# A hybrid decoder layer: score matmuls of differential attention on half-height stacks

## The chip, the cores and the metric

The kernel runs on one core of a Trainium2 chip. The metric is the device time of one execution in microseconds (us), given as the median of the runs.

## What is computed

One decoder layer over 1024 tokens of width 1024, all in float32. The rows are normalised, projected by one matrix `w_in`, and split among two groups of four heads. Group A is causal differential attention: each head has two components `c` with queries and keys of 64 features, two softmaxes, and the difference of the two weighs the values. Group B is retention in chunks of 128 tokens. The heads' outputs are normalised, gated, projected by `w_out`, normalised again and added to the input. The part that the change touches:

```python
s = jnp.einsum('bhcqd,bhckd->bhcqk', qb, kf)      # d = 64, c = 2 components
s = jnp.where(causal, s, jnp.float32(-1e30))
p = jax.nn.softmax(s, axis=-1)
a = p[:, :, 0] - lam * p[:, :, 1]
return jnp.einsum('bhqk,bhkv->bhqv', a, vf)
```

## The kernel before, in words

To keep float32 accuracy, most operands are split into a high part (rounded to the matmul's operand type) and a low part (the rest). The projections multiply high by high, high by low and low by high: three matmuls in `proj_rows` (L296 to L298, 256 columns each) and in `proj_cols` (L308 to L310, 512 columns each).

The projections run block by block: 16 blocks of 256 columns of `w_in`, each in four groups (`main_group`). After each group the program emits other work of the heads ("side" functions): `attend(i)` of a differential head, which is `diff_scores` of query tile i and `diff_values` of tile i - 1, over the eight groups of two blocks; and `ret_chunks` of a retention head. A planner then orders the instructions of every engine by when it expects their operands and buffers to be ready, so the score matmuls stand between projection matmuls of later blocks. The order on an engine is fixed after that.

`diff_qk` makes the rotated queries and keys of one head, transposed: features in rows, tokens in columns. The tiles `hi` and `lo` (L373, L374) hold the parts, the queries' two components in rows 0-31 and 32-63, the keys' in 64-95 and 96-127, for the two rotary halves `r`. Sixteen transfers from SP (`mv`, L384 and L385) for each half of the tokens copy them into the stacks `st["q"]` and `st["k"]`. A stack has four row blocks of 32 for each component `u` and rotary half `r`: the queries as high, high, low, low, the keys as high, low, high, low. One matmul over the 128 rows thus adds all four products for one `r`, and two matmuls (L399, r = 0 and 1) make the scores of one component.

`diff_scores` for tile i has n = (i + 1) * 128 keys: one piece up to 512 keys, two equal pieces above. Each piece of each component takes one bank of the pool `ps_s` (3 banks). DVE finds the largest score (L403 with the mask, L408 without), ACT takes the exponential (L413) and so frees the bank, and DVE subtracts the two components (L426). `diff_values` transposes the difference (L444) into banks of the pool `ps_m` (`pm`, 3 banks), ACT copies them out (L447), and the matmuls L449 apply them to the values, in a `pm` bank that is held until the output is gated (`emit_y`, L343). `ret_chunks` uses three `pm` tiles in turn, and so do the transposes at the start (`norm_tile`, L278) and before the output projection (`prep_tile`, L566). The output projection (`out_tile`, L585 to L587) writes to banks of `ps_s` and of `ps_j` in turn.

Of the kernel before, what the change touches and what calls it, by code (L numbers as in the profile page):

```python
# [10 lines left out]
F32 = mybir.dt.float32  # L11
F32R = mybir.dt.float32r
# [5 lines left out]
PSUM = bass.MemoryType.PSUM  # L18
# [12 lines left out]

# Column layout of the constants that depend on shapes alone.
C_FREQ = 0
# [6 lines left out]

# Heads (differential 0-3, retention 4-7) and the order of their blocks of w_in:
# part 0 holds the values and gates, part 1 the queries and keys.
HEADS = [0, 4, 1, 5, 2, 6, 3, 7]
# [4 lines left out]
def shape_constants():  # L48
    c = np.zeros((P, NCST), np.float64)
    c[:, C_FREQ:C_FREQ + 64] = THETA ** (-np.arange(64) / 64.0)  # L50
    t = np.arange(S).reshape(NT, P).T
    for h in range(H):
        # Retention by g^(i-j) is g^(i+1) times a sum over values scaled by g^-(j+1).
        g = 1.0 - 2.0 ** (-5.0 - h)
        c[:, C_VSC + h * NT:C_VSC + (h + 1) * NT] = g ** (-(t + 1.0)) * 128.0 ** -0.5
        c[:, C_OSC + h * NT:C_OSC + (h + 1) * NT] = g ** (t + 1.0)
        c[:, C_RSC + h * NT:C_RSC + (h + 1) * NT] = g ** (t + 1.0) * 128.0 ** -0.5
    c[:64, C_QSC] = 64.0 ** -0.5
    c[64:, C_QSC] = 1.0
    return c.astype(np.float32)  # L60


def two_pi_parts():
    """1/(2 pi) times powers of two, modulo 1, in parts that multiply whole numbers exactly."""
    from fractions import Fraction

    inv = Fraction(1) / Fraction(
        "6.28318530717958647692528676655900576839433879875021164194988918461563281257")

    def turn(power):  # L70
        t = inv * power
        t -= round(t)
        return t

    def part(t, bits):
        q = Fraction(round(t * 2 ** bits), 2 ** bits)
        return float(q), t - q

    a = turn(2 ** 16)
    a1, r = part(a, 8)  # L80
    a2, r = part(r, 16)
    a3 = float(r)
    b = turn(2 ** 4)
    b1, r = part(b, 12)
    b2 = float(r)
    return a1, a2, a3, b1, b2, float(inv)


def body(ctx, tc, x, pos, wpk, wout, vecs, npre, npost, subln, cst, out):
# [18 lines left out]
    ps_j = pool("ps_j", 2, space=PSUM)  # L108
    ps_s = pool("ps_s", 3, space=PSUM)
    ps_m = pool("ps_m", 3, space=PSUM)  # L110

# [8 lines left out]

# [1 line left out]
    cs = const.tile([P, NCST], F32, name="cs")  # L122
# [9 lines left out]
    def rsqrt(dst, src, more):  # L132
        """(src + more) ** -0.5"""
        nc.vector.tensor_scalar(dst, src, more, None, op0=ALU.add)  # L134
        nc.gpsimd.tensor_tensor(dst, dst, halves[:, 0:dst.shape[-1]], op=ALU.pow)  # L135

# [1 line left out]
    NB = 16  # L138
    lo_turn = [0]

    def split_lo(dst, full, hi):
        """dst = full - hi, rounded to the tensor engine's operand (exact)."""
        lo_turn[0] += 1
        eng = nc.vector if lo_turn[0] % 4 in (2, 3) else nc.gpsimd
        eng.tensor_tensor(dst, full, hi.bitcast(F32), op=ALU.subtract)  # L145

    def load_chunk(b, c, staging=None):
        """A quarter of a block."""
        raw = (staging or wraw).tile([P, 2, 256], F32, tag="raw", name="raw")
        nc.sync.dma_start(raw, wpk[b, :, 2 * c:2 * c + 2, :])  # L150
        hi = whi.tile([P, 2, 256], F32R, tag="whi", name="whi")
        nc.scalar.copy(hi, raw)  # L152
        lo = wlo.tile([P, 2, 256], F32R, tag="wlo", name="wlo")
        split_lo(lo, raw, hi)
        return hi, lo
# [6 lines left out]

# [1 line left out]
    HT = S // 2  # L164
# [9 lines left out]
    def angles(tp, posi):  # L174
        """cos and sin of position * frequency, with an exact reduction to one turn."""
        a1, a2, a3, b1, b2, inv = two_pi_parts()
# [27 lines left out]
        nc.vector.tensor_tensor(C, C, B, op=ALU.subtract)  # L204
        # small parts first
        nc.vector.tensor_scalar(acc, A, a3 * 2.0 ** -16, None, op0=ALU.mult)
# [6 lines left out]
        frac(acc, acc, t2)  # L213
        # cos x = sin(x + a quarter turn)
        nc.vector.tensor_scalar(t1, acc, 0.25, None, op0=ALU.add)
# [69 lines left out]
    def proj_rows(w, t2):  # L285
        """Two token tiles of u @ block: [tok, 2, 256]."""
        ps = pj()
        for j in range(2):
            t = 2 * t2 + j
            dst = ps[:, j * 256:(j + 1) * 256]  # L290
            cols = slice(t % 4 * P, (t % 4 + 1) * P)
            for kt in range(KT):
                wh, wl = weight(w, kt)
                a = uh[t // 4][:, kt, cols]
                b = ul[t // 4][:, kt, cols]
                nc.tensor.matmul(dst, lhsT=a, rhs=wh, start=(kt == 0 and j == 0), stop=False)  # L296
                nc.tensor.matmul(dst, lhsT=a, rhs=wl, start=False, stop=False)  # L297
                nc.tensor.matmul(dst, lhsT=b, rhs=wh, start=False, stop=(kt == KT - 1 and j == 1))  # L298
        return ps.rearrange("p (j f) -> p j f", j=2)

    def proj_cols(w, f, half):
        """128 features of the block over 512 tokens, transposed."""
        ps = pj()
# [30 lines left out]
    def emit_y(st, t, o_ps, tot):  # L334
        """The head's output, normalised and gated, to its columns of y."""
        hh, gt = st["h"], st["g"]
# [10 lines left out]

# [1 line left out]
    dp = {}  # L349
# [4 lines left out]
    def diff_qk(st, w, g):  # L354
        """Step g of 4: features (first, second rotary halves) of each half of the tokens."""
        half, f = g // 2, g % 2
        if g == 0:
            st["q"] = dp["stk"].tile([P, 2, 2, S], F32R, tag="qs", name="qs")
            st["k"] = dp["stk"].tile([P, 2, 2, S], F32R, tag="ks", name="ks")
        sl = slice(half * HT, (half + 1) * HT)  # L360
# [14 lines left out]
        for r, o in enumerate((o1, o2)):  # L375
            nc.scalar.copy(hi[:, r, :], o)
            split_lo(lo[:, r, :], o, hi[:, r, :])
        for u in range(2):
            for b in range(4):
                rows = slice(b * 32, (b + 1) * 32)  # L380
                q0, k0 = u * 32, 64 + u * 32
                sq = hi if b < 2 else lo
                sk = hi if b % 2 == 0 else lo
                mv(st["k"][rows, u, :, sl], sk[k0:k0 + 32, :, :])  # L384
                mv(st["q"][rows, u, :, sl], sq[q0:q0 + 32, :, :])  # L385

    def diff_scores(st, i):
        n = (i + 1) * P
        pieces = [(0, n)] if n <= 512 else [(0, n // 2), (n // 2, n // 2)]
        np_ = len(pieces)  # L390
        probs, sums = [], []
        for u in range(2):
            nm = sm_.tile([P, 2], F32, tag="nm", name="nm")
            banks = []
            for b, (k0, kn) in enumerate(pieces):
                last = b == np_ - 1
                sp = ps_s.tile([P, 512], F32, tag="sc", name="sc")
                for r in range(2):
                    nc.tensor.matmul(sp[:, 0:kn], lhsT=st["q"][:, u, r, i * P:(i + 1) * P],  # L399
                                     rhs=st["k"][:, u, r, k0:k0 + kn], start=(r == 0), stop=(r == 1))  # L400
                if last:
                    # -(scores with the mask), and the least of it
                    nc.vector.tensor_tensor_reduce(  # L403
# [3 lines left out]
                else:  # L407
                    nc.vector.tensor_reduce(nm[:, 0:1], sp[:, 0:kn], axis=AX.X, op=ALU.max, negate=True)  # L408
                banks.append(sp)
            p = dp["pp"].tile([P, S], F32, tag="p", name="p")  # L410
            ss = sm_.tile([P, 2], F32, tag=f"ss{u}", name="ss")
            for b, (k0, kn) in enumerate(pieces):
                nc.scalar.activation(p[:, k0:k0 + kn], banks[b][:, 0:kn], AF.Exp,  # L413
                                     scale=-1.0 if b == np_ - 1 else 1.0,
                                     bias=nm[:, np_ - 1:np_], accum_out=ss[:, b:b + 1])
# [40 lines left out]

# [1 line left out]
    def ret_qk(st, w, t2):  # L458
# [63 lines left out]

# [1 line left out]
    fp = {}  # L524
# [8 lines left out]
    def split_wout(nh, ms):  # L533
        """Rows of w_out for half nh of the columns, scaled by what y was not yet scaled by."""
        for m in ms:
# [63 lines left out]

# [1 line left out]
    heads = [{"h": hh} for hh in HEADS]  # L601
# [53 lines left out]

    # Blocks in the order of their weights, and what follows each group of four.
    def attend(i):
# [63 lines left out]
def pack(inputs):  # L721
    """The inputs, laid out for the program's loads."""
    w = np.asarray(inputs["w_in"])[0]
# [49 lines left out]
```

## Time and profile before

| what | value |
|---|---|
| median of 3 runs | 607.66 us (607.46 to 608.18) |
| span of the profiled execution, first to last instruction | 606.4 us |
| TensorE (PE) busy | 588.3 us, 97% |
| VectorE (DVE) busy | 324.4 us, 53% |
| ScalarE (ACT) busy | 236.1 us, 39% |
| GpSimd (POOL) busy | 140.7 us, 23% |
| mean granted clock of TensorE | 0.999 of full speed |

The profile gives the span of its execution; the execution's own time is not listed apart from those of the timed runs, whose median lies 1.3 us above the span. PE are the matmuls, PEld the loads of their stationary operand, which run beside them. Successive matmuls overlap in the profile, so their durations add up to more than the time that they take; the chain of work that ended last, which follows each step back to what released it, gives each matmul only the time that it added.

### The profile page before, as it was taken

What the parts mean: (1) busy time and instruction counts of PE and PEld (TensorE: products, weight loads), DVE (VectorE), ACT (ScalarE), POOL (GpSimd) and SP (SyncE); (2) the same over time, 40 slices, a digit from 0 to 9 for tenths busy, and PEclk for the clock granted to TensorE, in tenths of its full rate; (3) what the DMA queues carried; (4) which work ended last, traced back from release to release, by engine and by line L of the source; (5) the groups of instructions that cost most, each with busy time, mean ns of one, the idle gap of its engine ahead of it and who ended that gap; (6) DMA issues with size and microseconds to landing.
All of it is one profiled execution on the core that took longest, in us unless ns stands there. A gap on an engine that the chain in (4) does not pass through costs nothing.

```text
span 606.4 us, 10873 instructions
## 1 busy us (share of the span) xinstructions
PE 588.3 (97%) x4144; PEld 552.3 (91%) x4144; DVE 324.4 (53%) x820; ACT 236.1 (39%) x652; POOL 140.7 (23%) x171
## 2 busy tenths in 40 slices
PE   4999999999999999999999999999999999999995
PEld 3999989999989999999899998899999988888884
DVE  4888335755654357723444556456566673343232
ACT  5643522444433343534134445223546443212110
POOL 4303124411224032313241102343310230000000
PEclk9999999999999999999999999999999999999999
DMA  8602237510228420202185202482202372332221
GB/s 298 237 2 71 70 69 174 161 33 22 76 59 224 92 80 9 79 10 78 37 189 152 79 10 78 92 222 66 67 27 79 112 272 62 122 119 76 91 69 71
DMA packets 36196, 59.66 MB, mean 98 GB/s; under 512 B 4784, under 2 KB 12208, under 8 KB 36144
## 3 DMA queue, kind: packets, MB, share of 16 engines
q1 hardware_dynamic: 36000, 58.70, 33.0%
q8 instruction: 33, 0.54, 0.3%
q10 hardware_dynamic: 144, 0.26, 0.1%
q14 instruction: 19, 0.16, 0.1%
HBM read 34.30 MB, written 7.86 MB: 70 GB/s over the span
## 4 chain that ended last, share of the span: by engine, by line
PE 95%; DVE 1%; DMA 1%; issue 1%; ACT 0%; POOL 0%; SPq 0%; DVEq 0%; POOLq 0%; ACTq 0%
PE pj L296 15%; PE pj L298 15%; PE pj L297 15%; PE sc L399 6%; PE pm L449 5%; PE pj L308 5%; PE pj L310 5%; PE pj L309 5%; PE pm L444 3%; PE pj L585 2%; PE op L585 2%; PE pj L587 2%; PE pj L586 2%; PE op L587 2%; PE op L586 2%; PE pm L566 1%
## 5 line engine op out<-in xcount | busy, mean ns | idle before, releaser
L296 PE MATMUL pj<-whi,uh 128*128 128x256 f32 x768 | 221.6, 289 | 1.0 <-ACT uh L281 1.0
L298 PE MATMUL pj<-whi,ul 128*128 128x256 f32 x768 | 221.1, 288 | 0.5 <-DVE ul L282 0.5
L297 PE MATMUL pj<-wlo,uh 128*128 128x256 f32 x768 | 219.9, 286 | 0.0
L296 PEld LDWEIGHTS pj<-whi,uh 128*128 128x128 f32 x768 | 148.1, 193 | 2.1 <-ACT uh L281 1.6
L298 PEld LDWEIGHTS pj<-whi,ul 128*128 128x128 f32 x768 | 148.0, 193 | 1.0 <-DVE ul L282 0.8
L297 PEld LDWEIGHTS pj<-wlo,uh 128*128 128x128 f32 x768 | 148.1, 193 | 0.6
L135 POOL TENSOR_TENSOR tot<-tot,halves 128x1 f32<-128x1 f32 (+1 forms) x56 | 34.5, 616 | 275.3 <-DVE tot L134 273.2
L413 ACT ACTIVATE p<-sc,nm 128x384 f32<-128x384 f32 (+5 forms) x96 | 55.1, 580 | 53.8 <-DVE nm L403 52.5
L145 POOL TENSOR_TENSOR wlo<-raw,whi 128x512 fp32r<-128x512 f32 x32 | 46.4, 1453 | 78.5 <-ACT whi L152 68.8
L152 ACT CAST whi<-raw 128x512 fp32r<-128x512 f32 x64 | 39.4, 623 | 34.3 <-PE pj L309 17.5
L308 PE MATMUL pj<-uh,whi 128*128 128x512 f32 x128 | 50.5, 394 | 0.0
L309 PE MATMUL pj<-ul,whi 128*128 128x512 f32 x128 | 50.4, 394 | 0.0
L310 PE MATMUL pj<-uh,wlo 128*128 128x512 f32 x128 | 50.2, 392 | 0.0
L399 PE MATMUL sc<-ks,qs 128*128 128x384 f32 (+5 forms) x192 | 46.1, 346 | 0.0
L449 PE MATMUL pm<-v,at 128*128 128x128 f32 x288 | 39.7, 275 | 0.0
L447 ACT COPY at<-pm 128x512 f32<-128x512 f32 (+3 forms) x48 | 23.1, 481 | 42.4 <-PE pm L444 42.3
L449 PEld LDWEIGHTS pm<-v,at 128*128 128x128 f32 x288 | 36.8, 192 | 0.6
L145 DVE TENSOR_TENSOR wlo<-raw,whi 128x512 fp32r<-128x512 f32 x32 | 26.1, 827 | 19.9 <-ACT whi L152 19.0
L343 DVE SCALAR_TENSOR_TENSOR y<-pm,tot,gt 128x128 f32<-128x128 f32 x56 | 18.4, 348 | 24.9 <-POOL tot L135 16.6
L399 PEld LDWEIGHTS sc<-ks,qs 128*128 128x128 f32 x192 | 30.5, 191 | 1.0
L403 DVE CUSTOM_DVE_ANT_0 sc<-sc,mask,nm 128x320 f32<-128x320 f32 (+3 forms) x32 | 21.0, 655 | 18.8 <-PE sc L399 18.6
L434 ACT ACTIVATE sq<-pm,cs 128x128 f32<-128x128 f32 x32 | 11.4, 363 | 47.5 <-PE pm L511 47.4
(145 smaller groups left out, 971.5 us busy)
## 6 DMA issues: line engine op xcount, KB each, us to landing
raw<-in_wpk SPq DMA_DIRECT2D x64, 256.0 KB, 3.4
xt<-in_x SPq DMA_DIRECT2D x15, 512.0 KB, 3.8
ks<-rhi SPq DMA_DIRECT2D x32, 128.0 KB, 2.4
qs<-rhi SPq DMA_DIRECT2D x32, 128.0 KB, 2.4
ks<-rlo SPq DMA_DIRECT2D x32, 128.0 KB, 2.4
qs<-rlo SPq DMA_DIRECT2D x32, 128.0 KB, 2.4
raw<-in_wout SPq DMA_DIRECT2D x16, 256.0 KB, 3.0
out<-ob SPq DMA_DIRECT2D x16, 256.0 KB, 2.4
```

The source lines that it names most:

```text
L135: nc.gpsimd.tensor_tensor(dst, dst, halves[:, 0:dst.shape[-1]], op=ALU.pow)
L145: eng.tensor_tensor(dst, full, hi.bitcast(F32), op=ALU.subtract)
L152: nc.scalar.copy(hi, raw)
L296: nc.tensor.matmul(dst, lhsT=a, rhs=wh, start=(kt == 0 and j == 0), stop=False)
L297: nc.tensor.matmul(dst, lhsT=a, rhs=wl, start=False, stop=False)
L298: nc.tensor.matmul(dst, lhsT=b, rhs=wh, start=False, stop=(kt == KT - 1 and j == 1))
L308: nc.tensor.matmul(ps, lhsT=wh, rhs=uh[half][:, kt, :], start=(kt == 0), stop=False)
L309: nc.tensor.matmul(ps, lhsT=wh, rhs=ul[half][:, kt, :], start=False, stop=False)
L310: nc.tensor.matmul(ps, lhsT=wl, rhs=uh[half][:, kt, :], start=False, stop=(kt == KT - 1))
L399: nc.tensor.matmul(sp[:, 0:kn], lhsT=st["q"][:, u, r, i * P:(i + 1) * P], rhs=st["k"][:, u, r, k0:k0 + kn], start=(r == 0), stop=(r == 1))
L413: nc.scalar.activation(p[:, k0:k0 + kn], banks[b][:, 0:kn], AF.Exp, scale=-1.0 if b == np_ - 1 else 1.0, bias=nm[:, np_ - 1:np_], accum_ou ...
L449: nc.tensor.matmul(o_ps[:, 0:P], lhsT=at[:, j * P:(j + 1) * P], rhs=v[:, j0 + j, :], start=(j0 + j == 0), stop=(j0 + j == i))
```

## The change

The stacks hold each part once: four tiles of 128 rows by 1024 tokens (queries high, queries low, keys high, keys low), with component 0 in rows 0-63 and component 1 in rows 64-127, both rotary halves within these. There are still 16 transfers for each half of the tokens, of half the size. The scores of one component are now three matmuls over its 64 rows (high by high, low by high, high by low; the product of the low parts is left out), and the matmuls of the two components alternate, each component in a bank of its own. For each piece of the keys both components are now done before the next piece; the exponentials follow behind all of the maxima. The pool `ps_s` has 4 banks in place of 3, and `ps_m` 2 in place of 3. The rest of the diff is comments.

```diff
-    ps_s = pool("ps_s", 3, space=PSUM)
-    ps_m = pool("ps_m", 3, space=PSUM)
+    ps_s = pool("ps_s", 4, space=PSUM)
+    ps_m = pool("ps_m", 2, space=PSUM)
...
         if g == 0:
-            st["q"] = dp["stk"].tile([P, 2, 2, S], F32R, tag="qs", name="qs")
-            st["k"] = dp["stk"].tile([P, 2, 2, S], F32R, tag="ks", name="ks")
+
+            for n in ("qh", "ql", "kh", "kl"):
+                st[n] = dp["stk"].tile([P, S], F32R, tag=n, name=n)
...
-        for u in range(2):
-            for b in range(4):
-                rows = slice(b * 32, (b + 1) * 32)
-                q0, k0 = u * 32, 64 + u * 32
-                sq = hi if b < 2 else lo
-                sk = hi if b % 2 == 0 else lo
-                mv(st["k"][rows, u, :, sl], sk[k0:k0 + 32, :, :])
-                mv(st["q"][rows, u, :, sl], sq[q0:q0 + 32, :, :])
+        for n, src in (("h", hi), ("l", lo)):
+            for r in range(2):
+                for u in range(2):
+                    rows = slice(64 * u + 32 * r, 64 * u + 32 * r + 32)
+                    mv(st["q" + n][rows, sl], src[32 * u:32 * u + 32, r, :])
+                    mv(st["k" + n][rows, sl], src[64 + 32 * u:96 + 32 * u, r, :])
...
+        qs = slice(i * P, (i + 1) * P)
+        nms, banks = [], ([], [])
         for u in range(2):
-            nm = sm_.tile([P, 2], F32, tag="nm", name="nm")
-            banks = []
-            for b, (k0, kn) in enumerate(pieces):
-                last = b == np_ - 1
-                sp = ps_s.tile([P, 512], F32, tag="sc", name="sc")
-                for r in range(2):
-                    nc.tensor.matmul(sp[:, 0:kn], lhsT=st["q"][:, u, r, i * P:(i + 1) * P],
-                                     rhs=st["k"][:, u, r, k0:k0 + kn], start=(r == 0), stop=(r == 1))
+            nms.append(sm_.tile([P, 2], F32, tag="nm", name="nm"))
+        for b, (k0, kn) in enumerate(pieces):
+            last = b == np_ - 1
+            sps = [ps_s.tile([P, 512], F32, tag="sc", name="sc") for u in range(2)]
+            terms = (("qh", "kh"), ("ql", "kh"), ("qh", "kl"))
+            for m, (qn, kn_) in enumerate(terms):
+                for u in range(2):
+                    rows = slice(64 * u, 64 * u + 64)
+                    nc.tensor.matmul(sps[u][:, 0:kn], lhsT=st[qn][rows, qs], rhs=st[kn_][rows, k0:k0 + kn],
+                                     start=(m == 0), stop=(m == 2))
+            for u in range(2):
+                sp, nm = sps[u], nms[u]
...
-                banks.append(sp)
+                banks[u].append(sp)
+        for u in range(2):
+            nm = nms[u]
             p = dp["pp"].tile([P, S], F32, tag="p", name="p")
...
-                nc.scalar.activation(p[:, k0:k0 + kn], banks[b][:, 0:kn], AF.Exp,
+                nc.scalar.activation(p[:, k0:k0 + kn], banks[u][b][:, 0:kn], AF.Exp,
```

## Rows read from the trace of the kernel before

**Rows 1.** Page, busy time of each engine, share of the span, instructions.

```profile
PE 588.3 (97%) x4144; PEld 552.3 (91%) x4144; DVE 324.4 (53%) x820; ACT 236.1 (39%) x652; POOL 140.7 (23%) x171
```

**Rows 2.** Page, the chain that ended last, by engine and by line.

```profile
PE 95%; DVE 1%; DMA 1%; issue 1%; ACT 0%; POOL 0%; SPq 0%; DVEq 0%; POOLq 0%; ACTq 0%
PE pj L296 15%; PE pj L298 15%; PE pj L297 15%; PE sc L399 6%; PE pm L449 5%; PE pj L308 5%; PE pj L310 5%; PE pj L309 5%; PE pm L444 3%; PE pj L585 2%; PE op L585 2%; PE pj L587 2%; PE pj L586 2%; PE op L587 2%; PE op L586 2%; PE pm L566 1%
```

**Rows 3.** What PE waited for: us in total, times, longest.

```profile
PE pm L278 <- DVE xu L272: 8.0, 2, 7.1
...
PE pm L486 <- ACT qkT L483: 0.6, 1, 0.6
```

**Rows 4.** Score matmuls by shape, whole kernel: busy us, mean ns.

```profile
L399 PE MATMUL sc<-ks,qs 128*128 128x512 f32 x48 | 14.6, 403 | 0.0
...
L399 PE MATMUL sc<-ks,qs 128*128 128x128 f32 x16 | 2.5, 257 | 0.0
```

**Rows 5.** The chain in order of time: start us, us, what; steps of each width.

```profile
by line: PE pj L296 15.0%; PE pj L298 15.0%; PE pj L297 15.0%; PE sc L399 5.6%; PE pm L449 5.3%; PE pj L308 4.8%; PE pj L310 4.8%; PE pj L309 4.8%; PE pm L444 2.6%; PE pj L585 2.4%; PE op L585 2.4%; PE pj L587 2.4%; PE op L587 2.4%; PE pj L
...
103.50 0.48 PE sc L399 x4
110.07 0.70 PE sc L399 x4
...
126.19 0.88 PE sc L399 x6
...
135.77 1.04 PE sc L399 x6
...
194.20 0.40 PE sc L399 x4
194.59 0.17 PE pj L296
...
214.07 0.93 PE sc L399 x4
...
452.27 1.22 PE sc L399 x6
...
463.29 1.39 PE sc L399 x6
```

**Rows 6.** Weight loads and matmuls in time, 193.9 to 194.6 us, 128-column scores.

```profile
193.92 0.54 PEld L399 LDWEIGHTS sc<-ks,qs 128*128 128x128 f32 x4
194.37 0.19 PEld L296 LDWEIGHTS pj<-whi,uh 128*128 128x128 f32 x1
...
194.03 0.56 PE L399 MATMUL sc<-ks,qs 128*128 128x128 f32 x4
```

**Rows 7.** PE in time, 159.8 to 160.5 us, transposes then projection.

```profile
159.83 0.60 PE L444 MATMUL pm<-ident,p 128*128 128x128 f32 x4
160.18 0.48 PE L309 MATMUL pj<-ul,whi 128*128 128x512 f32 x1
160.50 0.40 PE L310 MATMUL pj<-uh,wlo 128*128 128x512 f32 x1
```

**Rows 8.** ACT copy by shape; engines from 480 us; the chain near 496 us.

```profile
L447 ACT COPY at<-pm 128x512 f32<-128x512 f32 x24 | 14.1, 587 | 17.5 <-PE pm L444 17.4
...
480.00:500.00 20.00, 18.57 (x158) 18.18 (x157) 15.62 (x35) 10.60 (x24) 6.72 (x10) 1.00 0.67 231
...
496.39 0.37 ACT sq L434
...
499.89 0.66 PE pm L566 x4
```

**Rows 9.** One stack's transfers (KB, us to landing); waits for the staging tiles.

```profile
ks<-rhi SPq DMA_DIRECT2D x32, 128.0 KB, 2.4
...
DVE rlo L145 <- DMA qs<-rlo: 7.6, 2, 4.3
...
ACT rhi L376 <- DMA ks<-rhi: 6.2, 2, 3.5
```

## The prediction

> **What bounds the kernel now.** I read the engine totals first [rows 1]: TensorE (PE) is busy 588.3 us of a span of 606.4, every other engine at most 53%. Busy is not bound by itself, so the chain of waits comes next [rows 2]: 95% of the chain that ended last is PE, and the score matmuls (L399) have 6% of it (the same chain in order of time says 5.6%, that is 34.0 us [rows 5]). The last view is what PE waited for [rows 3]: its largest entry is 8.0 us in two waits at the start, for a normalised tile; in the middle of the kernel it practically never waits, because projection matmuls of the next blocks fill every hole. So a microsecond of PE's own work, added or removed between 97 and 472 us, should show in the end nearly one for one. A faster transfer or a faster DVE there should show as nothing.
>
> All prices below come from the one profiled execution (span 606.4). The three timed runs have a median of 607.66, so 1.3 us lie around the span; I add differences to 607.66.
>
> **What a score matmul costs today.** The mean durations in the table by shape (403 ns at 512 columns) [rows 4] are not prices: successive matmuls overlap. The price is the share on the chain [rows 5]: four of 512 columns take 0.93 us, six take 1.39, so 0.232 each; 448: 1.22/6 = 0.203; 384: 1.04/6 = 0.173, or 0.70/4 = 0.175; 320: 0.88/6 = 0.147; 256: 0.48/4 = 0.12. For 128 columns the row says 0.40 for four, but the projection matmul behind them takes 0.17 in place of its usual 0.12, so four cost 0.45: 0.1125 each. From 256 to 512 columns the price falls by 0.11 us; from 256 to 128 only by 0.008. Something else is the floor there, and the weight loads show it: four loads begin at 193.92, the next at 194.37, that is 0.1125 us per load [rows 6]. A matmul of few columns is paced by its load.
>
> Per head, one step with each of 128, 256, 384 and 512 columns has four matmuls, and the four two-piece steps (320, 384, 448, 512) have eight: 0.45 + 0.48 + 0.70 + 0.93 + 1.18 + 1.38 + 1.62 + 1.86 = 8.60 us; four heads: 34.4 us, against 34.0 on the chain. The table by shape has six such groups (48, 48, 32, 32, 16 and 16 matmuls, 192 in all), of which the first and the last stand in [rows 4].
>
> **What the change does to them.** Each (piece, component) gets three matmuls over 64 rows in place of two over 128: 288 in place of 192, with the same columns each. Every load still brings 128 columns. What two matmuls on different halves of the rows cost together, no row shows; I bound it.
> - Lower end: the two run fully side by side and all loads are hidden. A pair costs one old matmul; three pairs replace four: 3/4 of 34.4 = 25.8, so -8.6 us.
> - Upper end: they run one after the other. Six replace four: 51.6, so +17.2 us.
> - Between: the columns run side by side, but loads still come one after another at 0.1125 us [rows 6]. A piece then has six load slots, and its last matmul must still stream its columns. One-piece steps: 128 columns 6 x 0.1125 = 0.675 (+0.225); 256: 5 x 0.1125 + 0.12 = 0.68 (+0.20); 384: 0.74 (+0.04); 512, where a pair of slots (0.225) is just under one stream (0.232): 2 x 0.232 + 0.1125 + 0.232 = 0.81 (-0.12). Two-piece steps, twelve slots in a row: 320: 11 x 0.1125 + 0.147 = 1.38 (+0.20); 384: 1.41 (+0.03); 448: 1.44 (-0.18); 512: 5 x 0.232 + 0.345 = 1.50 (-0.36). Sum per head +0.04, four heads +0.2 us.
>
> I take the middle value: the only floor that the trace shows under a small matmul is the load, and the change puts more loads on fewer streamed columns. The gain at 448 and 512 is eaten at 128 to 320.
>
> The Trainium skill, "TensorE: Matmul & The Clock Gate", section LDWEIGHTS, says the same of the loads: the time goes by the columns, and 32 rows take as long as 128. Its section on packing small matmuls also has loads to different row groups overlap; were that so here, the sum would be at the lower end. The rows before show only full-height loads, so they cannot tell.
>
> **Going in and out of 64-row work.** Each step's matmuls form a burst among 128-row matmuls: 32 steps, at least 64 changes. Changes between kinds of PE work that the trace has cost nothing: four transposes at 159.83 and one 512-column matmul behind them last until 160.50, 0.67 us, and 4 x 0.109 + 0.232 = 0.67 [rows 7]. The most a change could cost, by the rows, is that the array empties: 403 ns for one matmul less its 232 ns price, 0.17 us [rows 4, 5]. Bounds: 0 to 64 x 0.17 = 10.9 us; a gain is excluded, because a change takes no work away. I take 0, the value of the nearest rows, and treat the upper part as a rival.
>
> **PSUM banks.** The pool `pm` goes from three banks to two, the score pool from three to four. Four score banks let all twelve matmuls of a two-piece step stand together; today the third bank splits them into two to six. Worth nothing by itself, as PE has other work meanwhile. Two `pm` banks are tighter: `diff_values` from i = 4 on holds its output bank while two groups of transposes pass through, and a retention chunk uses three tiles in turn. Uncovered, 16 second transposes and 16 chunks would each wait for one ACT copy (0.587 us for 512 columns [rows 8]): 18.8 us. Nearly all of it is covered by the projection matmuls of each group (24 of 0.232 us or 48 of 0.12, over 5.5 us), which the planner moves in front. If that cover is gone, as at the passage to the output projection (PE busy 18.57 of the 20 us from 480, and a chain of ACT and DVE work from 496.39 until the transposes at 499.89 [rows 8]), one or two waits come out. I take +0.5 us, range 0 to 3; a gain is excluded, since a bank less can start nothing earlier.
>
> **Transfers and the rest.** SP still issues 16 transfers per half and head, 128 in all, now of 64 KB in place of 128 KB [rows 9]. They hide behind PE's projections now and will do so after. ACT and DVE wait 6.2 and 7.6 us for the staging tiles to be read out [rows 9]; halved bytes may halve that, but neither is on the chain. The queue order on SP behind these transfers (weight loads, head outputs) is unchanged. DVE now finds the maxima of both components before ACT starts the exponentials of the first; PE waits for neither. Price of all this: 0, with the projections as cover.
>
> **Sum.** +0.2 (matmuls) + 0 (changes of height) + 0.5 (banks) = +0.7: 608.4 us.
>
> **Rivals.**
> 1. Loads overlap too, or are fetched ahead for the other half: up to -8.6, with the banks' 0.5 some -8: about 599.6; partly so, 600 to 606. For it: the load of the next matmul already starts while the present one runs (194.37, under the burst that starts at 194.03 [rows 6]). Against: at 128 columns they do not get under 0.1125.
> 2. Emptying the array at each change, slower: 64 x 0.17 on top of the forecast: 608.4 + 10.9 = 619.3; it decides against the change from 0.02 us per change (1.2 us in all). For it: the results of a 128-row matmul come out late (0.17 us), and a half-height one may not overtake them. Against: other changes of kind cost nothing [rows 7]. The Trainium skill has this as a rule: "TensorEngine Tiling (Array Packing)", section Key Properties, says that changing the tiling mode, not just the tile, drains TensorE. No run here shows it yet; it gives no duration.
> 3. The change does not do what it says: the halves run one after another. 607.66 + 17.2 + 0.5 = 625.4. For it: no two matmuls in the trace before start closer than 0.11 us. Against: all of those use all rows, so they could not.
> 4. Rivals 1 and 2 together: -8.6 + 10.9 + 0.5, about 610.5; smaller prices of a change leave it anywhere between 600 and 610.
>
> **How the numbers follow.** Forecast 35% (606 to 611: same 20, slower 13, faster 2); loads overlapping 25% (faster); emptying the array 16% (slower); one after another 14% (slower); both 10% (faster 6, same 2, slower 2). A measurement here can tell 0.2%, 1.2 us, from no change. Faster 0.33, same 0.22, slower 0.45. Range: the lower end at the whole gain, 599.5; the upper end takes in the emptied array with some of the banks' cost, 621. Outside are the serial case (14%) and a few per cent below. The forecast's own range is 606 to 611.
>
> **What would show it.** Forecast right: L399 has 288 matmuls, the two of a pair start about 0.11 us apart, a group of three pairs of any width up to 448 takes some 0.7 us on the chain, and L399 keeps 5.5 to 6% of it. Rival 1: pairs start together, L399 falls to about 4.3%. Rival 2: a hole of 0.1 to 0.2 us, or a late first matmul, at each entry and exit of a burst, so the projection matmul behind a burst costs more than 0.12. Rival 3: starts 0.15 to 0.23 us apart following the width, L399 at 8%. Banks: new waits of PE for `pm` readers (ACT L447, L483, DVE L343). I am wrong altogether if PE's idle time grows by more than 3 us, since then something other than the score matmuls decides.

## The result, and the profile after

The changed kernel takes 633.93 us (median; 632.38 to 634.59) against 607.62 us of the kernel before on the same chip: 4.2% slower, ratio 1.0424 with a 95% interval of 1.0409 to 1.0440. The forecast was 608.4 with a range of 599.5 to 621.0; the time lies above it. The profiled execution took 633.96 us, with a span of 632.2.

The page of the changed kernel: busy time of each engine, and the chain that ended last by engine and by line.

```profile
PE 604.9 (96%) x4240; PEld 548.1 (87%) x4240; DVE 325.4 (51%) x820; ACT 238.1 (38%) x652; POOL 136.2 (22%) x171
...
PE 91%; DVE 2%; DMA 2%; ACT 1%; issue 1%; POOL 1%; SPq 0%; DVEq 0%; POOLq 0%; ACTq 0%
PE pj L296 14%; PE pj L297 14%; PE pj L298 14%; PE sc L402 6%; PE pm L456 5%; PE pj L308 5%; PE pj L310 5%; PE pj L309 5%; PE pm L451 3%; PE op L592 2%; PE op L593 2%; PE op L594 2%; PE pj L594 2%; PE pj L593 2%; PE pj L592 2%; DMA raw<-in_wpk 2%
```

Against [rows 1, 2]: PE still dominates the chain, but with 91% in place of 95%; some 57 us of the span are now on other things, against 30. Some 17 of these 27 us stand before 75 us, where the chain goes over transfers and DVE beside a PE that is mostly busy, so the shares do not yet price anything. The score matmuls (now L402) have 6.0% of 632.2 in the list by time, 37.9 us, against 34.0. So 4 us of 26 stand on the line where I looked for them.

What PE waited for in the changed kernel (us in total, times, longest), to be set beside [rows 3], and PE's busy time in three stretches (length, PE, PEld, DVE, ACT, POOL busy with instructions, granted clock, share of the DMA engines, GB/s):

```profile
PE pm L278 <- DVE xu L272: 7.3, 1, 7.3
PE pj L298 <- DVE ul L282: 2.6, 3, 1.8
PE pm L493 <- ACT qkT L490: 2.3, 3, 1.0
PE pm L517 <- DVE yt L343: 1.8, 1, 1.8
...
0.00:60.00 60.00, 46.42 (x357) 44.50 (x358) 44.76 (x80) 29.48 (x61) 16.73 (x25) 1.00 0.47 162
60.00:500.00 440.00, 439.47 (x3264) 403.08 (x3263) 230.58 (x631) 177.74 (x511) 106.74 (x123) 1.00 0.21 63
500.00:540.00 40.00, 33.71 (x210) 29.26 (x209) 17.39 (x42) 12.81 (x32) 6.59 (x11) 0.91 0.42 143
```

PE has holes at two edges: at the start, and at the passage to the output projection, where 6.3 of 40 us are idle (before, in the row from 480 us of [rows 8], 1.4 of 20). Behind these holes the granted clock is at 0.50, the lower of its two levels (1.2 GHz), from 523.0 to 529.8 us. Between the edges PE is busy all the time and yet later. Two marks in PE's order tell where the time went. The first matmul of `proj_cols` (L308) starts at 69.59 before and 72.77 after: +3.2 us. The first matmul of the output projection starts at 501.4 (L585) and 524.2 (L592): 19.6 us more between the marks, of which 5.4 are larger holes (PE is idle for 6.8 us between them, 1.4 before); 14.2 us are PE's own. From there to the end: 105.0 and 108.0, +3.0. The sum is 25.8, the difference of the spans.

The bursts themselves. The chain of the changed kernel in order of time (start us, us, what):

```profile
100.47 0.48 PE sc L402 x6
100.95 0.32 PE pj L296
...
113.67 0.72 PE sc L402 x6
114.39 0.26 PE pm L451
...
221.67 0.89 PE sc L402 x6
...
229.46 1.07 PE sc L402 x12
230.53 0.58 PE pm L451 x4
```

and the weight loads of the first burst:

```profile
100.40 0.19 PEld L402 LDWEIGHTS sc<-kh,qh 64*128 64x128 f32 x2
100.51 0.19 PEld L402 LDWEIGHTS sc<-kh,ql 64*128 64x128 f32 x2
100.62 0.19 PEld L402 LDWEIGHTS sc<-kl,qh 64*128 64x128 f32 x2
```

The loads come two per 0.11 us, one for each half: they overlap, and so do the matmuls. Six of 512 columns take 0.89 us (six serial would be 1.39), twelve of 320 take 1.07 (eight full-height ones take 1.18 by [rows 5]). But what follows pays: a projection matmul right behind a burst takes 0.32 in place of 0.12, four transposes 0.58 in place of 0.44. And three pairs of 128 columns should take 3 x 0.11 = 0.34, but the burst takes 0.48. Going in and coming out both cost.

### The profile page after: what moved, and what is told of

It reads as the page before. It is cut to its first block, busy times and chain, and to the rows that moved or that the text cites. A ratio compares the mean times of both kernels' runs of the same rounds, so it can differ in the third digit from the quotient of the medians.

```text
span 632.2 us, 11135 instructions
## 1 busy us (share of the span) xinstructions
PE 604.9 (96%) x4240; PEld 548.1 (87%) x4240; DVE 325.4 (51%) x820; ACT 238.1 (38%) x652; POOL 136.2 (22%) x171
## 3 DMA queue, kind: packets, MB, share of 16 engines
q1 hardware_dynamic: 31904, 50.31, 25.1%
## 4 chain that ended last, share of the span: by engine, by line
PE 91%; DVE 2%; DMA 2%; ACT 1%; issue 1%; POOL 1%; SPq 0%; DVEq 0%; POOLq 0%; ACTq 0%
PE pj L296 14%; PE pj L297 14%; PE pj L298 14%; PE sc L402 6%; PE pm L456 5%; PE pj L308 5%; PE pj L310 5%; PE pj L309 5%; PE pm L451 3%; PE op L592 2%; PE op L593 2%; PE op L594 2%; PE pj L594 2%; PE pj L593 2%; PE pj L592 2%; DMA raw<-in_wpk 2%
## 5 line engine op out<-in xcount | busy, mean ns | idle before, releaser
L145 POOL TENSOR_TENSOR wlo<-raw,whi 128x512 fp32r<-128x512 f32 x32 | 43.4, 1355 | 85.9 <-ACT whi L152 45.6
L308 PE MATMUL pj<-uh,whi 128*128 128x512 f32 x128 | 50.5, 395 | 0.0
L310 PEld LDWEIGHTS pj<-uh,wlo 128*128 128x128 f32 x128 | 24.1, 188 | 5.1 <-issue 0.4
L308 PEld LDWEIGHTS pj<-uh,whi 128*128 128x128 f32 x128 | 24.1, 188 | 5.0 <-issue 0.4
L309 PEld LDWEIGHTS pj<-ul,whi 128*128 128x128 f32 x128 | 24.1, 188 | 4.6
```

Of the source, the lines that this page charges most:

```text
L308: nc.tensor.matmul(ps, lhsT=wh, rhs=uh[half][:, kt, :], start=(kt == 0), stop=False)
L309: nc.tensor.matmul(ps, lhsT=wh, rhs=ul[half][:, kt, :], start=False, stop=False)
L310: nc.tensor.matmul(ps, lhsT=wl, rhs=uh[half][:, kt, :], start=False, stop=(kt == KT - 1))
```

## The experiments

Two theories were left by this trace: A, the missing `ps_m` bank (the edges), and B, the changes between 64-row and 128-row work (the middle). C, matmuls that run one after another (rival 3), is priced beside them. Each ratio is against the kernel before on the same chip, whose median there was 607.62 to 608.12 us. In the diffs, `...` marks what is left out. A "burst" below is a run of 64-row matmuls without a 128-row one between, counted in PE's order in the trace.

**The banks, one change at a time.** Three banks in each pool, with the half-height matmuls:

```diff
-    ps_s = pool("ps_s", 4, space=PSUM)
-    ps_m = pool("ps_m", 2, space=PSUM)
+    ps_s = pool("ps_s", 3, space=PSUM)
+    ps_m = pool("ps_m", 3, space=PSUM)
```

> The changed kernel with three banks in each pool (ps_s 3, ps_m 3), as before the change; the half-height score matmuls stay. Theory A (the missing ps_m bank costs most of the 26 us): the holes at the start (40 to 60 us) and at the passage to the output projection (500 to 530 us) close, and 608 to 614 us are left: the score matmuls' own share of the chain grew by 4 us (6.0% of 632.2 against 5.6% of 606.4). Theory B (going in and out of 64-row work costs it: emptied array, rival 2 of the prediction): the time stays above 625 us. Theory C (mostly serial, rival 3): above 624 us too, with starts 0.15 to 0.23 us apart.

Measured: 639.19 us, ratio 1.0503 (1.0486 to 1.0521). That is slower than the changed kernel, by 5 us, and far from 608 to 614: theory A alone falls. The edges did close: L308 starts at 69.04 and 106.1 us lie behind the first output matmul, but 463.0 us lie between the marks, 31.2 more than before. The list by time gives L402 8.3% of the chain, 53 us of 638.2. The chain shows why:

```profile
236.85 0.72 PE sc L402 x3
237.57 0.31 PE pj L296
...
238.59 0.71 PE sc L402 x3
239.31 0.31 PE pj L297
```

Three matmuls of 384 columns, of one component only, take 0.72 us; in the changed kernel six of the same width, both components, take 0.72. With three banks the planner finds a bank for one component, runs its three matmuls, and goes back to projections. There are 70 bursts (36 of them three matmuls long) against 51 in the changed kernel, and 34 of the 36 hold one component alone. Of the 288 matmuls 140 start without one of the other half beside them, against 24 in the changed kernel. Theory C has its time, but not its reason: they are not serial by nature, they stand alone.

The other half of the change, only the banks, in the kernel before:

```diff
-    ps_s = pool("ps_s", 3, space=PSUM)
-    ps_m = pool("ps_m", 3, space=PSUM)
+    ps_s = pool("ps_s", 4, space=PSUM)
+    ps_m = pool("ps_m", 2, space=PSUM)
```

> The kernel before with only the banks moved (ps_s 4, ps_m 2). Theory A: 625 to 632 us, with the holes of the changed kernel at the start and at the passage. Theories B and C: 607 to 610 us, as the prediction priced the banks at 0 to 3 us.

Measured: 628.33 us, ratio 1.0334 (1.0281 to 1.0388; the runs scatter from 624.75 to 633.13). As theory A said. Its profile (span 625.3) has PE's holes and the clock lowered behind them, in the same columns as above:

```profile
0.00:60.00 60.00, 45.72 (x340) 43.96 (x341) 45.21 (x80) 29.18 (x59) 14.84 (x25) 0.97 0.45 153
480.00:520.00 40.00, 30.96 (x225) 27.93 (x225) 23.33 (x58) 18.38 (x49) 9.36 (x14) 0.94 0.42 145
```

and PE in order of time there, with the idle time ahead of an instruction and who ended it:

```profile
505.46 1.16 PE L449 MATMUL pm<-v,at 128*128 128x128 f32 x8 [0.73 <-ACT at L447]
...
507.79 0.71 PE L486 MATMUL pm<-qkT 128*128 128x128 f32 x4 [0.73 <-ACT qkT L483]
...
514.82 0.49 PE L510 MATMUL pm<-rR,qkT 128*128 128x128 f32 x2 [1.82 <-DVE yt L343]
```

The work in `pm` banks has slipped behind the last projection, where nothing covers its copies any more: 83 matmuls stand between the last one of the projections and the first of the output projection, 24 in the kernel before. The marks: L308 at 74.72 (+5.1), 443.2 us between (+11.4), 107.4 to the end (+2.4). So each half of the change costs 20 to 31 us by itself, and both together 26: the fourth score bank is what lets the pairs meet, and the bank that it is taken from is what keeps the edges closed.

**Does the order of the pairs matter?** As the first run, but component 0's three matmuls first:

```diff
-            for m, (qn, kn_) in enumerate(terms):
-                for u in range(2):
+            for u in range(2):
+                for m, (qn, kn_) in enumerate(terms):
```

> As the run with three banks each, but the three matmuls of component 0 come first and then the three of component 1, so neighbours share their rows, save one pair of neighbours in each six. If pairs of different rows run side by side, this must cost more than the run with three banks each: of six matmuls only the two in the middle can overlap, so five columns' times in place of three, about 2/3 more matmul time: 34.4 x 0.75 = 25.8 becomes 43, some 17 us more. If pairs run one after another anyway, no difference.

Measured: 640.18 us, ratio 1.0525 (1.0509 to 1.0541), no difference from 639.19. My expectation of 17 us was wrong. It also tells less than I meant, as with three banks most of the pairs were parted anyway (70 bursts, 37 of three). The next run settles the question.

**The matmuls by themselves.** Behind the last output tile of the kernel before, stretches of matmuls of no use:

```diff
+        def pairs(n, k):
+            for m in range(3):
+                mm(b0, lo, n, (k + m) % 4)
+                mm(b1, up, n, (k + m + 1) % 4)
...
+        for k in range(24):
+            pairs(512, k)
+            full(512, k)
```

> The kernel before, with matmuls of no use behind its last output tile (about 900, some 150 us), in stretches: half-height pairs alone, full-height matmuls alone, and bursts of three pairs with one full-height matmul between, for 512, 256 and 128 columns; and one stretch with three matmuls on the same half, then three on the other. Side by side: a pair of 512 costs 0.23 us, serial 0.46. Loads one after another: a pair of 128 columns costs 0.225 us; overlapped: 0.11. A change of height costing nothing: a burst of three pairs and a full matmul of 512 takes 4 x 0.23 = 0.92 us; emptied array at both changes: 1.1 to 1.3 us.

PE in order of time (start us, us, line, output and input, rows, shape, count); of repeated bursts the first stands:

```profile
613.71 16.64 PE L729 MATMUL b<-jt 64*128 64x512 f32 x144
630.28 5.76 PE L729 MATMUL bf<-jt 128*128 128x512 f32 x24
635.96 0.97 PE L729 MATMUL b<-jt 64*128 64x512 f32 x6
636.86 0.50 PE L729 MATMUL bf<-jt 128*128 128x512 f32 x1
637.29 0.96 PE L729 MATMUL b<-jt 64*128 64x512 f32 x6
...
667.89 16.69 PE L729 MATMUL b<-jt 64*128 64x512 f32 x144
684.51 5.76 PE L729 MATMUL bf<-jt 128*128 128x512 f32 x24
690.20 8.26 PE L729 MATMUL b<-jt 64*128 64x128 f32 x144
698.38 2.89 PE L729 MATMUL bf<-jt 128*128 128x128 f32 x24
701.21 0.55 PE L729 MATMUL b<-jt 64*128 64x128 f32 x6
701.69 0.33 PE L729 MATMUL bf<-jt 128*128 128x128 f32 x1
701.95 0.55 PE L729 MATMUL b<-jt 64*128 64x128 f32 x6
```

- 72 pairs of 512 columns take 630.28 - 613.71 = 16.57 us, 0.230 a pair: what one full-height matmul takes. The pair costs nothing over a single one.
- 72 pairs of 128 columns: 698.38 - 690.20 = 8.18 us, 0.114 a pair. The loads of the two halves overlap; the full-height floor of 0.1125 per load [rows 6] holds for a pair, not for each of its loads.
- Three pairs and one full matmul in turn: 637.29 - 635.96 = 1.33 us, where 4 x 0.23 = 0.92 would do. Two changes of height cost 0.41 us. With 128 columns 0.74, against 4 x 0.114 = 0.46: 0.28 us.
- Three on one half, then three on the other, over and over: 684.51 - 667.89 = 16.62 us for 144, the same 0.23 a pair. In a long row the order doesn't matter; what matters is that the partner is there to be run.
- With 256 columns, once the granted clock is full again (1.00 from 732 us), a pair takes 0.119 us, and three pairs and one full matmul 0.87 where 4 x 0.119 = 0.48 would do: 0.39 us for two changes.

The weight loads of the stretch with 512 columns show what a change consists of:

```profile
635.42 0.19 PEld L729 LDWEIGHTS bf<-jt 128*128 128x128 f32 x1
635.96 0.53 PEld L729 LDWEIGHTS b<-jt 64*128 64x128 f32 x6 [0.35 <-issue]
636.86 0.19 PEld L729 LDWEIGHTS bf<-jt 128*128 128x128 f32 x1 [0.37 <-issue]
```

In a row of one height the load for the next matmul starts together with the matmul ahead of it (both at 635.42), and its 0.11 us ([rows 6]) are hidden. At a change it comes late: going in, 0.32 us after the start of the last full matmul (635.65), and going out, 0.32 us after the start of the last pair (636.54). That is 0.1 us more than the 0.23 us of a matmul, and the load's own 0.11 us then lie open. So going in and coming out cost about the same, 0.2 us each.

**No shortage of banks.** One pool of six banks for all that `ps_s` and `ps_m` held, in the changed kernel, and the same in the kernel before:

```diff
-    ps_s = pool("ps_s", 4, space=PSUM)
-    ps_m = pool("ps_m", 2, space=PSUM)
+    ps_x = pool("ps_x", 6, space=PSUM)
```

> The changed kernel with one pool of six banks for the scores and all that ps_m holds, so that neither is short by itself. Theory now: two causes of about 12 us each, changes of height (51 bursts of 64-row matmuls, 0.4 us each, 20 us, less 8.6 us from matmuls side by side) and the ps_m bank (the rest). Then 617 to 623 us are left here. If the ps_m bank were all of it, 608 or less; if changes of height were all, 630 or more.

> The kernel before with the same pool of six banks. The kernel before hardly waits for banks, so 606 to 609 us; it is the kernel that the changed one with six shared banks is compared with.

Measured: 615.94 us, ratio 1.0135 (1.0120 to 1.0150), a little under the 617 to 623 expected, and 607.31 us, ratio 0.9994 (0.9985 to 1.0003). The edges are closed (the first matmul of `proj_cols` at 68.48, 104.3 us behind the first output matmul), pairs meet, and 38 bursts are left, 11 of them with all twelve matmuls of a step. The half-height work by itself then costs 615.94 - 607.31 = 8.6 us. By the prices of the stretches: 38 x 0.41 = 15.6 us for the changes, less the 8.6 us of the lower end of my sum, 7.0, so 1.6 us are left unexplained.

**Half height against full height, same count.** As the first run (three banks each), but each of the 288 matmuls over all 128 rows:

```diff
-                    rows = slice(64 * u, 64 * u + 64)
+                    rows = slice(0, P)
```

> The changed kernel with three banks in each pool, but each of the 288 score matmuls goes over all 128 rows of the stacks (the scores then add both components, which changes what is computed). Nothing runs side by side and no height changes. If matmul time were the cost, this is the dearest: 34.4 x 1.5 = 51.6 us, 17 more than before. If changes of height are the cost: 608 + 17 = 625 us, below the 639 of the half-height run with the same banks.

Measured: 624.72 us, ratio 1.0298 (1.0274 to 1.0323); L402 has 8.2% of 622.3, 51.0 us, beside the 51.6 worked out. Half-height matmuls in the same places cost 14.5 us more than full-height ones, although they do half of the work (PE's order is the same in both but for two matmuls): it is the changes, not the matmuls.

**Where the two banks hurt.** The changed kernel, with the transposes of the start, of the angles and of the output projection in score banks:

```diff
-            ps = pm()
+            ps = psx()
...
+    def psx():
+        return ps_s.tile([P, 512], F32, tag="sc", name="sx")
```

> The changed kernel (ps_s 4, ps_m 2), with the transposes at the start, those of the angles and those before the output projection in banks of ps_s, which are idle then. If the ps_m bank costs at these two edges (holes of PE at 20 to 60 and at 500 to 530 us), 618 to 626 us; if it costs inside the attention work, 632 to 635 us.

Measured: 623.56 us, ratio 1.0267 (1.0252 to 1.0282), 10.4 us less than the changed kernel with the same 51 bursts. Most of the bank's cost is at the edges. To the 615.94 of six shared banks 7.6 us are left: 13 bursts more, which at 0.41 are 5.3 us, and some waits at the passage.

**More and fewer changes.** On six shared banks, three runs. The matmuls of query tiles 0 and 1, and of 2 and 3, in one burst:

```diff
+    def diff_scores(st, *steps):
+        made = [score_matmuls(st, i) for i in steps]
+        for i, m in zip(steps, made):
+            score_rest(st, i, *m)
...
-    dp["pp"] = dpool("pp", 3)
+    dp["pp"] = dpool("pp", 5)
```

> The changed kernel with six shared banks, the matmuls of query tiles 0 and 1 in one burst, and those of 2 and 3 (five probability buffers in place of three). Up to 8 bursts fewer than the 38 of the run with six shared banks. If each burst costs its two changes of height, 0.3 to 0.4 us: 615.9 - 8 x 0.35 = 613 us. If the changes cost nothing in the kernel: 616. Below 607 only if the side-by-side gain were held back by something else than the changes.

One full-height matmul of no use in the middle of each two-piece step (its bank is overwritten by the scores):

```diff
+            if b:
+                nc.tensor.matmul(sps[0][:, 0:P], lhsT=st["qh"][:, qs], rhs=st["kh"][:, 0:P], start=True, stop=True)
```

> The changed kernel with six shared banks and one full-height matmul of 128 columns of no use between the two pieces of each two-piece step: 16 matmuls and 32 changes of height more. By the stretches behind the output (0.29 to 0.41 us for two changes, 0.11 for the matmul): 16 x (0.4 to 0.52) = 6.4 to 8.3 us, so 622 to 624 us. If the changes cost nothing: 617.7.

And a half-height pair in its place:

```diff
+            if b:
+                for u in range(2):
+                    rows = slice(64 * u, 64 * u + 64)
+                    nc.tensor.matmul(sps[u][:, 0:P], lhsT=st["qh"][rows, qs], rhs=st["kh"][rows, 0:P], start=True, stop=True)
```

> The same with a half-height pair of 128 columns of no use in that place: the burst is longer, no change of height is added. 16 x 0.114 = 1.8 us: 617.7 by both theories; the difference to the run with the full-height matmul is the price of the 32 changes.

Measured, with the bursts counted:

| run | us | ratio (95%) | bursts |
|---|---|---|---|
| tiles 0 and 1, 2 and 3 together | 612.67 | 1.0079 (1.0064 to 1.0094) | 31 |
| six shared banks | 615.94 | 1.0135 (1.0120 to 1.0150) | 38 |
| a half-height pair added | 617.60 | 1.0160 (1.0145 to 1.0175) | 37 |
| a full-height matmul added | 624.47 | 1.0268 (1.0251 to 1.0285) | 53 |

The first and the third row came as expected, the last 0.5 us above its 622 to 624. A pair and a full matmul of 128 columns take the same time by themselves (8.18/72 and 2.83/24 us, both some 0.12), so the 6.87 us between the last two rows are the 16 bursts more: 0.43 us each, 0.21 for a change. Seven bursts fewer brought 3.3 us, 0.47 each. A two-piece step of 320 columns shows it on the chain. First with the full-height matmul (L398):

```profile
349.13 0.64 PE sc L403 x6
349.77 0.26 PE sc L398
350.02 0.64 PE sc L403 x6
```

then with the pair (L400):

```profile
346.05 0.64 PE sc L405 x6
346.69 0.06 PE sc L400 x2
346.75 0.49 PE sc L405 x6
```

Behind a half-height neighbour the second piece of 320 columns takes 0.49; behind a full-height one 0.64, and that one itself takes 0.26 where 0.12 would do.

No run beat the kernel before clear of noise. By an estimate from these prices, bursts of 0.43 us against a gain of 8.6 us at most, the scores would have to stand in fewer than 20 bursts, five for each head of eight query tiles; 31 is the least that I reached.

## Why the prediction was wrong, point by point

- **What bounds the kernel.** Right for the middle: PE's own work there came through one for one, as the run with 288 full-height matmuls shows (17.2 us more by the prices, 17.1 measured). It was incomplete for the edges, where PE has no projections left to move in front. The sign that I had named for being wrong altogether came: PE's idle time (span less busy) grew from 18.1 to 27.3 us.
- **The price of a pair.** The bounds were right, the value taken was not. I took one load after another (+0.2 us); the pairs ran at the lower end (0.230 for 512 columns, 0.114 for 128; -8.6 us when all meet). The rows of 128 columns showed a floor per load, but all of them were loads for the same rows, and I carried the floor over to loads for different rows. The Trainium skill, "TensorE: Matmul & The Clock Gate", in its part on packing small matmuls, has matmuls of different row groups run at the same time, and loads overlap matmuls in flight whose row group is another; the stretches agree (a pair in 0.230 and 0.114 us, the time of one full-height matmul). Two signs that I had named for the forecast came by accident: L402 kept 6.0% of the chain, and three pairs of 384 columns took 0.72 us. That is 3 x 0.174 us side by side and the 0.2 us of going in; the two of a pair start 0.003 us apart, the sign of rival 1, and not 0.11.
- **The price of a change of height.** This is the step that failed first. I took 0, from changes between transposes and matmuls [rows 7], which both use all rows; it is 0.2 us a change (0.41 and 0.43 for two, 0.28 where the matmuls have only 128 columns). My upper bound of 0.17 was a little low, as it priced the emptied array alone; the stretches show some 0.1 us of waiting and then a load of 0.11 us that nothing hides. I also took 64 changes; the planner made 102, as a step's matmuls do not always stand together. So rival 2, priced at 10.9 us, is 51 x 0.43 = 21.9 here. Rivals 1 and 2 together, which I had at 610.5 with 10%, are what happened, with the second twice as dear: the 14.2 us of PE's own in the middle are 21.9 less the part of the 8.6 that the matmuls standing in pairs brought. The Trainium skill's rule ("TensorEngine Tiling (Array Packing)", Key Properties: a change of the tiling mode, not of the tile, drains TensorE) agrees with the runs, which add the duration.
- **The banks.** The second failed step. I took 0.5 us, at most 3, with projections as cover. The cover holds in the middle. At the start, at the passage and in the first output matmuls, which ran at a lowered clock behind the holes, the changed kernel lost 3.2 + 5.4 + 3.0 = 11.6 us (with the 14.2 us of the middle, the whole 25.8), and the kernel before with the same banks 5.1 + 11.4 + 2.4 = 18.9, the difference of the spans. I had named the passage and seen its chain [rows 8], and priced it as one or two waits; but the work that two banks delay all along arrives there together. That two banks then let only one copy at a time run ahead is my reading of PE's waits in the kernel before with these banks (ACT L447 and L483), not a run of its own. With six shared banks 72 matmuls stand behind the last projection too, and PE is idle for only 2.7 us between the marks. The fourth score bank, which I put down as "worth nothing by itself", is worth 5 us at the least: with three banks each the pairs part, and the kernel takes 639.19 in place of 633.93, although its edges are closed.
- **Rival 3,** one after another, is refuted by the stretches, though the first run came to its time for another reason. Its support was a misreading as well: matmuls in the trace before do start closer than 0.11 us, as the transposes and the projection of [rows 7] show (four starts 0.11 apart from 159.83, and the next matmul at 160.18).
- **Transfers and the rest.** The bytes of the stacks halved (which takes SP's queue from 58.70 to 50.31 MB), and nothing came of it, as forecast: no transfer of the stacks appears among PE's waits.

What stays open: why the load at a change comes 0.1 us later than the matmul ahead would ask for was not tried; and how the 11.6 us at the edges split between the bank itself and the work delayed in the middle was not tried further than the run with the transposes in score banks.

## What to carry to other kernels

Matmuls on the two halves of the rows do run side by side, loads included, but each entry and each exit cost about 0.2 us here, so they pay only in long bursts: count the bursts in PE's order, not the matmuls. Both partners must have their banks at the same time, or the pair parts and the gain is gone. A PSUM bank taken from a pool that hardly seemed to need it is paid for where its cover ends, at the edges of the kernel; price it there.

## What the runs showed of the hardware that was not expected

Weight loads for different halves of the rows overlap fully: 0.114 us for a pair of 128 columns, the same as for one full-height load. In a long row of half-height matmuls the order of the halves is free: three and three takes 16.62 us where in turn takes 16.57, as if a matmul for idle rows did not wait for its predecessor on the other half; how, was not tried.

The granted clock can fall under a PE that the profile calls busy (the ends of matmuls are modelled there, so a busy PE is not PE at its peak). In the stretch with bursts of three pairs of 128 columns and one full matmul of 128 columns in turn, the first five bursts took 0.74 us each at full clock, and from 704.9 to 728.3 us 1.24 us each (the stretch until the fall, and the one behind it; columns as above):

```profile
701.20:704.90 3.70, 3.70 (x36) 2.97 (x35) 0.00 (x0) 0.00 (x0) 0.00 (x0) 0.99 0.00 0
704.90:728.30 23.40, 23.40 (x134) 18.97 (x133) 0.00 (x0) 0.00 (x0) 0.00 (x0) 0.50 0.01 1
```

That is the lower of its two levels, 1.2 GHz. The bursts with 512 columns kept the full clock, and so did the changed kernel's own scores between projections (1.00 from 60 to 500 us).
